# Neighbour sums on one core: the fourth group's first sums moved to the end of slot 4, and every result turned by VectorE

## The chip, the core and the metric

The kernel runs on one core of a Trainium2 chip. The metric is the device time of one execution in microseconds (us), taken as the median of several runs. The engines are TensorE (PE; its weight loads are listed apart as PEld), VectorE (DVE), ScalarE (ACT), GpSimd (POOL) and SyncE (SP, which here issues DMAs). Each engine runs its own instructions in the order in which the program lists them and waits on semaphores for what the others produce. SBUF is the on-chip memory, and PSUM holds the outputs of TensorE.

## The reference

For every edge, the feature row of its source node is added to the output row of its destination node. There are 4096 nodes with 128 features each in float32, and 65536 edges.

```python
output = np.zeros((num_nodes, dim), dtype=np.float32)
for i in range(len(edge_index_src)):
    output[edge_index_dst[i]] += node_features[edge_index_src[i]]
```

## The kernel before

**Tiling.** The nodes are 32 blocks of 128. The output is made in eight groups of 512 destinations (four blocks). For one group and one block of sources the kernel counts the edges between them in a 128 x 512 matrix `a`: DVE makes one-hot rows `oh` of the source and of the destination digits (`onehots`, line 804), PE multiplies them (`blocks`, line 817, into `psa`) and ACT copies the counts to SBUF (line 822). Then `product` (line 824) adds the block's features times `a` into `pso`, which holds 128 features x 512 destinations of the group; it takes two matmuls, since the features are split into a rounded part and a remainder. A **slot** is eight source blocks of one group, so a group has four slots and there are 32 slots (0 to 31).

**A slot on PE**, in order: `blocks` 0 to 3 of this slot, hook 2, `product` 4 to 7 of the slot before, `blocks` 4 to 7, hooks 3 and 4, `product` 0 to 3 of this slot, `finish`, hook 5. The one-hot rows of the next slot are written on DVE at the start of a slot, two buffers alternating: those of slot s + 2 need that the blocks of slot s are done, and PE cannot start slot s + 1 before DVE has written its rows.

**Sorting beside it.** The one-hot rows need the edges of each group sorted by source block. `pass2(g)` (line 625) does this for group g in steps hung on slots by a table of hooks (`at(slot, place, ...)`), so that they run between the slots of earlier groups: `buckets` (DVE, line 647), `chunk_sums` (POOL, lines 660 to 668, ends in the tile `four`), **`before_all`** (line 670: three matmuls of `four` with a triangular matrix into the PSUM tile `psb`, which ACT copies to `base`; these are the first sums that the title speaks of), `masked` and `folded` (POOL, multiply by `base` and add), `repeats` (DVE) and its folding (POOL), `ranks` (line 714: eight matmuls into `psr`, two ACT copies to `rank`), `permutations` (DVE, `p2a` or `p2c` from `rank`), `permuted` (PE, 48 matmuls `ps` of `p2a` with the payloads `v`), `take_pairs` (ACT) and `quad_keys` (DVE, the keys for the one-hot rows). `payloads` (POOL, `v`) of groups 2 to 6 is issued behind the next group's `chunk_sums`. `psb`, `psr` and `ps` share one PSUM buffer (tag `ps2`).

**At slot 4** two groups meet: hook 2 has `before_all`, `masked` and `folded` of group 3 (the fourth), hook 3 has `ranks` and `permutations` of group 2 (the third). Group 3's `buckets` and `chunk_sums` and group 2's `payloads` are hung on slot 2.

**Results.** When a group is complete, one slot later, ACT copies `pso` out (`evacuate`, line 375), and `finish` (line 391) turns it from features x destinations to destinations x features. For groups 0 and 2 (`BY_TENSOR`) PE turns it by four transposes into `psx`, ACT copies `psx` to `rows`, and one DMA of 256 KB stores it. For groups 1, 3, 4, 5 and 6 ACT copies `pso` to the PSUM tile `psx`, one DVE instruction turns its 32 x 32 blocks into `rows`, and four DMAs of 64 KB on SP's queue put the blocks in their places. Group 7 is turned at the very end (`leave`, line 408).

Of the kernel before, what the change touches and what calls it, by code (L numbers as in the profile page):

```python
# [8 lines left out]
P = 128  # L9
F32 = mybir.dt.float32  # L10
# [16 lines left out]
GROUPS = (4,) * 8  # L27
WARM = 38
LATE_PAYLOADS = (2, 3, 4, 5, 6)
BY_TENSOR = (0, 2)  # L30

WIN = ((0, 4, 0, 44), (4, 9, 0, 72), (9, 13, 8, 92), (13, 17, 16, 112), (17, NJ, 28, P))

# [44 lines left out]
def _fast(ctx, tc, X, src32, dst32, out, ident, fmax, flag_i, T):  # L78
    nc = tc.nc
    V, S, G, PE = nc.vector, nc.scalar, nc.gpsimd, nc.tensor  # L80
# [3 lines left out]
    sb1 = ctx.enter_context(tc.tile_pool(name="sb1", bufs=1))  # L84
    sb2 = ctx.enter_context(tc.tile_pool(name="sb2", bufs=2))
    ps = ctx.enter_context(tc.tile_pool(name="ps", bufs=2, space=bass.MemoryType.PSUM))
# [12 lines left out]
    for a, b in runs:  # L99
        at, n = 8 * sum(QN[:a]), 4 * QN[a]  # L100
        for queue, of, to in ((nc.sync, dst32, rawd), (nc.scalar, src32, raws)):
            queue.dma_start(
                out=to.rearrange("p (q n) w -> p q n w", q=NQ)[:, a:b, :n],
                in_=bass.AP(of, at, [[2 * T, P], [2 * n, b - a], [2, n], [1, 2]]))
# [268 lines left out]
    done = []  # L373

    def evacuate(k, pso):
        if k in BY_TENSOR:
            res = sb1.tile([P, 512], F32, name="res", tag="K1")
        else:
            res = ps.tile([P, 512], F32, name="psx", tag="misc", bufs=1)
        S.copy(out=res[:], in_=pso[:])  # L380
        done.append((k, res))

    def store_blocks(queues, rows, k):

        for a in range(4):
            queues[a % len(queues)].dma_start(
                out=out[4 * k * P:4 * (k + 1) * P, 32 * a:32 * (a + 1)].rearrange(
                    "(b j) f -> j b f", j=32),
                in_=rows[32 * a:32 * (a + 1)].rearrange("p (b f) -> p b f", f=32))

    def finish():
        for k, res in done:
            if k not in BY_TENSOR:
                rows = sb2.tile([P, 512], F32, name="rows", bufs=1)
                V.transpose(out=rows[:], in_=res[:])
                store_blocks((nc.sync,), rows, k)
                continue
            psx = ps.tile([P, 512], F32, name="psx", tag="misc", bufs=1)
            for i in range(4):
                PE.transpose(psx[:, i * P:(i + 1) * P], res[:, i * P:(i + 1) * P], ident[:])  # L400
            rows = sb2.tile([P, 4, P], F32, name="rows", bufs=1)
            S.copy(out=rows[:].rearrange("p i f -> p (i f)"), in_=psx[:])
            nc.sync.dma_start(
                out=out[4 * k * P:4 * (k + 1) * P, :].rearrange("(i p) f -> p i f", p=P),
                in_=rows[:])
        done.clear()

    def leave(k, pso):
# [209 lines left out]
    def at(slot, where, *fs):  # L618
        hooks.setdefault((slot, where), []).extend(fs)
# [5 lines left out]
    def pass2(g):  # L625
# [164 lines left out]
        f = 4 * g  # L790
        first_step = {3: (2, 4), 4: (6, 1)}.get(g, (f - 11, 1))
        at(*first_step, buckets, chunk_sums, owed.pop(g - 1, lambda: None))
        at(f - 8, 2, before_all, masked, folded)
        if g in LATE_PAYLOADS:
            owed[g] = payloads
        else:
            at(f - 8, 2, payloads)
        at(f - 7, 1, repeats, repeats_folded)
        at(f - 4, 5, ranks)
        at(f - 3, 1, lambda: permutations(0), lambda: permutations(1))  # L800
# [44 lines left out]
    def flag_of_all(fall):  # L845
# [3 lines left out]
                               op=OP.not_equal)  # L849

    buckets_1, payloads_1, column_sums_1, sums_1, counts_1 = pass2(1)
    buckets_2, chunk_sums_2 = pass2(2)
    for g in range(3, len(GROUPS)):
        pass2(g)

    V.tensor_copy(out=earlier[:, :, :4 * (NH - 1)].bitcast(F32),
                  in_=ones[:, :4 * (NH - 1)].bitcast(F32)[:, None].to_broadcast([P, 2, 2 * (NH - 1)]))
# [39 lines left out]
    for slot in range(slots):  # L897
# [21 lines left out]
        if slot > 1:  # L919
            for k in range(4, 8):  # L920
                product(k, *prev)
            if prev[0] % 4 == 3:
                evacuate(prev[0] // 4, prev[2])
# [4 lines left out]
        for k in range(4, 8) if slot == 0 else range(4):  # L928
            product(k, slot, a, pso)
        finish()  # L930
        do(slot, 5)
        prev = (slot, a, pso)
# [97 lines left out]
```

## Time and profile before

| what | value |
|---|---|
| median of 3 runs | 271.87 us (271.3 to 271.88) |
| profiled execution, its own time | 271.77 us |
| its span, first to last instruction | 270.2 us |
| PE busy | 252.3 us (93%) |
| DVE busy | 242.1 us (90%) |
| POOL busy | 197.0 us (73%), nothing after 212 us |
| ACT busy | 189.4 us (70%) |
| mean granted TensorE clock | 0.981 |

The last slots are PE's alone: PE works without a gap there. Earlier PE, DVE and POOL are all close to full, and which of them is waited for changes from slot to slot, so the table's shares do not say what a shorter piece of work is worth; the rows of the waits in order of time do.

### The profile page before, as it was taken

The numbers are of one execution on the slowest core, as the hardware profiler recorded it, in microseconds if no ns is written. First come the engines' busy times: TensorE is split into PE (matmuls) and PEld (weight loads), VectorE is DVE, ScalarE is ACT, GpSimd is POOL, SyncE is SP. The second block draws the span as 40 slices with busy tenths as digits, with TensorE's granted clock in tenths as the row PEclk, the third lists the DMA queues.
The fourth block names the chain that finished last, engine by engine and source line by source line (L and its number), as shares of the span: only waits on it lengthen the run. The fifth ranks groups of instructions, "written<-read, shape, count | busy, mean of one in ns | idle before, by whom it ended". The sixth has DMA issues, their size and how long they took to land.

```text
span 270.2 us, 7501 instructions
## 1 busy us (share of the span) xinstructions
PE 252.3 (93%) x3155; PEld 210.7 (78%) x3156; DVE 242.1 (90%) x270; ACT 189.4 (70%) x435; POOL 197.0 (73%) x205
## 2 busy tenths in 40 slices
PE   7899998989993999999899999999999999999991
PEld 7789997757882788778788887887888888878780
DVE  7999988999999199999999999999999989979801
ACT  3799898488763476676668687766876685868760
POOL 6499999999999996699999998999799300000000
PEclk9999999999998699999999999999999999999997
DMA  6910000000000010001000100200020020002002
GB/s 156 290 26 6 2 6 2 2 0 4 0 4 0 2 39 2 0 12 29 2 0 2 39 5 0 41 2 0 0 41 2 1 41 1 4 0 41 0 1 42
DMA packets 19556, 5.74 MB, mean 21 GB/s; under 512 B 12864, under 2 KB 19520, under 8 KB 19520
## 3 DMA queue, kind: packets, MB, share of 16 engines
q1 hardware_dynamic: 17648, 4.59, 7.7%
q10 hardware_dynamic: 1872, 0.66, 1.2%
q8 instruction: 25, 0.41, 0.6%
q14 instruction: 11, 0.09, 0.1%
HBM read 3.15 MB, written 2.10 MB: 19 GB/s over the span
## 4 chain that ended last, share of the span: by engine, by line
PE 54%; POOL 18%; DVE 17%; ACT 7%; issue 2%; DVEq 0%; POOLq 0%; ACTq 0%
PE pso L827 29%; PE psa L820 14%; DVE oh L242 10%; POOL cum L703 5%; ACT cum L284 4%; POOL xr L231 3%; POOL two L667 2%; POOL v L656 2%; PE ps L736 2%; PE psm L365 2%; PE psw L145 2%; POOL cum L710 1%; DVE oh L647 1%; POOL four L667 1%; DVE p2c L242 1%
## 5 line engine op out<-in xcount | busy, mean ns | idle before, releaser
L822 ACT CAST a<-psa 128x512 fp32r<-128x512 f32 x256 | 131.8, 604 | 31.8 <-PE psa L820 31.5
L827 PE MATMUL pso<-a,xr 128*128 128x512 f32 x512 | 136.3, 408 | 0.1
L827 PEld LDWEIGHTS pso<-a,xr 128*128 128x128 f32 x512 | 92.1, 191 | 17.4 <-ACT a L822 0.8
L242 DVE TENSOR_TENSOR oh<-psi,slo 128x4096 bf16<-128x4096 uint16 (+2 forms) x38 | 73.8, 1943 | 1.5 <-PE psa L820 1.5
L242 DVE TENSOR_TENSOR oh<-psi,dlo 128x4096 bf16<-128x4096 uint16 (+2 forms) x38 | 73.9, 1945 | 0.0
L820 PE MATMUL psa<-oh 128*128 128x128 bf16 x1024 | 68.8, 220 | 3.6 <-DVE oh L242 3.5
L820 PEld LDWEIGHTS <-oh 128*128 128x128 bf16 x1024 | 58.2, 98 | 17.7 <-issue 11.3
L656 POOL TENSOR_TENSOR v<-oh,sa 128x512 bf16<-128x512 bf16 x42 | 42.6, 1048 | 0.0
L703 POOL TENSOR_TENSOR cum<-oh,base 128x512 bf16<-128x512 bf16 x36 | 40.5, 1161 | 2.4 <-ACT base L678 2.4
L340 POOL TENSOR_TENSOR v<-oh,kab 128x704 f32<-128x704 bf16 x24 | 32.8, 1401 | 5.6 <-ACT kab L218 5.3
L242 DVE TENSOR_TENSOR p<-psi,rank 128x352 bf16<-128x352 uint16 (+5 forms) x60 | 26.0, 500 | 1.8 <-ACT rank L305 1.7
L667 POOL TENSOR_TENSOR two<-oh 128x512 bf16<-128x512 bf16 x18 | 20.4, 1160 | 4.2 <-DVE oh L647 4.2
L365 PE MATMUL psm<-v,p 128*128 128x64 bf16 x512 | 19.6, 193 | 0.9 <-DVE p L242 0.7
L242 DVE TENSOR_TENSOR p2a<-psi,rank 128x3072 bf16<-128x3072 uint16 (+2 forms) x14 | 14.2, 1062 | 5.9 <-ACT rank L724 5.9
L284 ACT ACTIVATE cum<-psc,sums 128x256 bf16<-128x256 f32 x50 | 19.1, 553 | 0.5 <-PE psc L281 0.5
L365 PEld LDWEIGHTS <-p 128*128 128x128 bf16 x512 | 17.1, 98 | 2.1 <-DVE p L242 1.7
L242 DVE TENSOR_TENSOR p2c<-psi,rank 128x3072 bf16<-128x3072 uint16 x8 | 13.6, 1745 | 0.0
L279 PE MATMUL psc<-early,oh 128*128 128x256 bf16 x67 | 13.2, 272 | 0.0
L647 DVE TENSOR_TENSOR oh<-psi,sbk 128x3072 bf16<-128x3072 uint16 (+3 forms) x9 | 12.5, 1393 | 0.0
L281 PE MATMUL psc<-early,oh 128*128 128x128 bf16 x67 | 12.1, 219 | 0.0
L710 POOL TENSOR_TENSOR cum<-cum 128x384 int32<-128x384 int32 x12 | 11.9, 1012 | 0.0
L535 ACT COPY ps<-ps 64x128 f32<-64x128 f32 x8 | 1.9, 235 | 13.8 <-issue 12.2
(117 smaller groups left out, 245.8 us busy)
## 6 DMA issues: line engine op xcount, KB each, us to landing
xf<-in_node_features_dram SPq DMA_DIRECT2D x4, 512.0 KB, 6.1
out_dram<-rows SPq DMA_DIRECT2D x22, 64.0 KB, 2.0
out_dram<-rows SPq DMA_DIRECT2D x2, 256.0 KB, 2.3
raw<-in_edge_index_src_dram ACTq DMA_DIRECT2D x1, 336.0 KB, 5.4
raw<-in_edge_index_dst_dram SPq DMA_DIRECT2D x1, 336.0 KB, 5.6
raw<-in_edge_index_src_dram ACTq DMA_DIRECT2D x2, 88.0 KB, 2.4
raw<-in_edge_index_dst_dram SPq DMA_DIRECT2D x2, 88.0 KB, 2.6
out_dram<-rows ACTq DMA_DIRECT2D x2, 64.0 KB, 2.9
```

The source lines that it names most:

```text
L242: V.tensor_tensor(out=dst.rearrange("p i (m k) -> p i m k", k=2), in0=io.rearrange("p i (m k) -> p i m k", k=2), in1=keys2[:, :, None, :]. ...
L284: S.activation(out=cum[:, 2 * i:2 * i + 2].rearrange("p j e -> p (j e)"), in_=psc[:, 2 * i * P:2 * (i + 1) * P], func=RELU, bias=bias)
L340: G.tensor_tensor(out=v1[q][:, l::4], in0=oh1q(q)[:, l::4], op=OP.mult, in1=kab[:, q, l::4, None].to_broadcast([P, NJ, NB]))
L365: PE.matmul(out=psm[:, l * 64:(l + 1) * 64], lhsT=t[:, j, l % 2, :], rhs=v1[q][:, 4 * j + l].bitcast(BF16), start=j == 0, stop=j == n - 1)
L647: V.tensor_tensor(out=T2["o"][:, c0:c1], op=OP.is_equal, in0=psi[:, 2].bitcast(U16).rearrange("p (s k) -> p s k", k=4)[:, None].to_broadca ...
L656: G.tensor_tensor(out=T2["v"][:, c:c + 4], in0=T2["o"][:, c:c + 4], op=OP.mult, in1=sa[:, c:c + 4, None, d0:d0 + 4].to_broadcast([P, 4, NB ...
L667: G.tensor_tensor(out=to[:, js], in0=of[:, js, 0], in1=of[:, js, 1], op=OP.add)
L703: G.tensor_tensor(out=flat("c")[:, c:c + 4], in0=flat("o")[:, c:c + 4], op=OP.mult, in1=T2["b"][:, c // NH, None].to_broadcast([P, 4, P]))
L710: G.tensor_tensor(out=t[:, cs, :n], in0=t[:, cs, :n], in1=t[:, cs, n:2 * n], op=OP.add)
L820: PE.matmul(out=psa[:, i * P:(i + 1) * P], lhsT=oh[:, 0, 4 * k + i, :], rhs=oh[:, 1, 4 * k + i, :], start=True, stop=True)
L822: S.copy(out=a[:, k, :], in_=psa[:])
L827: PE.matmul(out=pso[:], lhsT=xr[s // 16][:, s % 16, v, :], rhs=a[:, k, :], start=s == 0 and v == 0, stop=s == NB - 1 and v == 1)
```

## The change

`BY_TENSOR` and the branch for it are taken out of `evacuate` and `finish`: the results of groups 0 and 2 now go the way of the others (ACT copies to the PSUM tile `psx`, DVE turns, four DMAs of 64 KB). And for group 3 alone `before_all`, `masked` and `folded` move from hook 2 to hook 5 of slot 4.

```diff
-BY_TENSOR = (0, 2)
@@ evacuate
-        if k in BY_TENSOR:
-            res = sb1.tile([P, 512], F32, name="res", tag="K1")
-        else:
-            res = ps.tile([P, 512], F32, name="psx", tag="misc", bufs=1)
+        res = ps.tile([P, 512], F32, name="psx", tag="misc", bufs=1)
         S.copy(out=res[:], in_=pso[:])
         done.append((k, res))
@@ finish
         for k, res in done:
-            if k not in BY_TENSOR:
-                rows = sb2.tile([P, 512], F32, name="rows", bufs=1)
-                V.transpose(out=rows[:], in_=res[:])
-                store_blocks((nc.sync,), rows, k)
-                continue
-            psx = ps.tile([P, 512], F32, name="psx", tag="misc", bufs=1)
-            for i in range(4):
-                PE.transpose(psx[:, i * P:(i + 1) * P], res[:, i * P:(i + 1) * P], ident[:])
-            rows = sb2.tile([P, 4, P], F32, name="rows", bufs=1)
-            S.copy(out=rows[:].rearrange("p i f -> p (i f)"), in_=psx[:])
-            nc.sync.dma_start(
-                out=out[4 * k * P:4 * (k + 1) * P, :].rearrange("(i p) f -> p i f", p=P),
-                in_=rows[:])
+            rows = sb2.tile([P, 512], F32, name="rows", bufs=1)
+            V.transpose(out=rows[:], in_=res[:])
+            store_blocks((nc.sync,), rows, k)
@@ pass2
-        at(f - 8, 2, before_all, masked, folded)
+        after_sums = (f - 8, 5 if g == 3 else 2)
+        at(*after_sums, before_all, masked, folded)
         if g in LATE_PAYLOADS:
             owed[g] = payloads
         else:
-            at(f - 8, 2, payloads)
+            at(*after_sums, payloads)
```

The line numbers of the changed kernel are 1 lower up to `evacuate` and 13 or 14 lower behind `finish`. POOL's instructions keep their order.

PE in slot 4, before, from the last matmul of blocks 0 to 3 on (`psb` first sums, `pso` products, `psr` rank sums, `psx` the turned result of group 0):

```order
L820 MATMUL psa<-oh 128x128
L676 LDWEIGHTS before
L676 MATMUL psb<-four_2056,before 128x256
...
L827 MATMUL pso<-a,xr_177 128x512 x8
...
L720 MATMUL psr_2231<-same_1822,identb 128x96
L827 MATMUL pso<-a,xr_176 128x512 x8
L400 MATMUL psx<-ident,res 128x128 x4
L820 LDWEIGHTS oh
```

PE at the same place of the changed kernel:

```order
L807 MATMUL psa<-oh 128x128
L814 MATMUL pso<-a,xr_177 128x512 x8
...
L706 MATMUL psr_2214<-same_1822,identb 128x96
L814 MATMUL pso<-a,xr_176 128x512 x8
L662 LDWEIGHTS before
L662 MATMUL psb<-four_2056,before 128x256
...
L807 LDWEIGHTS oh
```

The first sums stand behind the rank sums and the last products of the slot, ahead of the first weights of slot 5, and the four transposes are gone.

ACT from slot 4 to slot 5, before (`a` are the counts' copies, `res` and `rows` the two copies of group 0's result):

```order
L822 CAST a<-psa 128x512 x12
L678 CAST base_2180<-psb 128x256
L380 COPY res<-pso 128x512
L822 CAST a<-psa 128x512 x4
L724 CAST rank_457<-psr_2231 128x96 x2
L402 COPY rows<-psx 128x512
L822 CAST a<-psa 128x512 x8
```

and in the changed kernel:

```order
L809 CAST a<-psa 128x512 x12
L376 COPY psx<-pso 128x512
L809 CAST a<-psa 128x512 x4
L710 CAST rank_457<-psr_2214 128x96 x2
L664 CAST base_2241<-psb 128x256
L809 CAST a<-psa 128x512 x8
```

The copy of the first sums stands behind the two rank copies, and one copy of the result is gone.

DVE from the rows of slot 5 to those of slot 6, before (`p2a` is the permutation of group 2):

```order
L242 TENSOR_TENSOR oh<-psi,slo_2077 128x4096
L242 TENSOR_TENSOR oh<-psi,dlo_2078 128x4096
L242 TENSOR_TENSOR p2a<-psi,rank_457 128x3072 x2
L242 TENSOR_TENSOR oh<-psi,slo_2077 128x4096
L242 TENSOR_TENSOR oh<-psi,dlo_2078 128x4096
```

and in the changed kernel:

```order
L241 TENSOR_TENSOR oh<-psi,slo_2077 128x4096
L241 TENSOR_TENSOR oh<-psi,dlo_2078 128x4096
L241 TENSOR_TENSOR p2a<-psi,rank_457 128x3072 x2
L390 STREAM_TRANSPOSE rows<-psx 128x512
L241 TENSOR_TENSOR oh<-psi,slo_2077 128x4096
L241 TENSOR_TENSOR oh<-psi,dlo_2078 128x4096
```

A turn stands ahead of the rows of slot 6; a second one, of group 2's result, stands in the same way ahead of the rows of slot 14.

## Rows read from the trace of the kernel before

**Rows 1.** Chain that ended last: start us, us, engine, output, line, count.

```profile
88.70 3.41 PE pso L827 x8
...
93.34 0.34 PE psr L720 x8
...
95.60 0.44 PE psx L400 x4
96.03 0.89 PE psa L820 x16
96.93 1.90 PE pso L827 x8
...
99.73 0.72 PE ps L736 x24
...
180.72 4.49 DVE oh L242 x2
185.26 1.07 PE psa L820 x16
```

**Rows 2.** Timeline of PE, slot 4: start, us, ..., count, [idle before, releaser].

```profile
82.51 1.07 PE L820 MATMUL psa<-oh 128*128 128x128 bf16 x16 [0.42 <-DVE oh L242]
87.90 0.80 PE L676 MATMUL psb<-four,before 128*128 128x256 bf16 x3 [4.32 <-POOL four L667]
```

**Rows 3.** Stretches: length, busy us (instructions) by engine, PEclk, DMA share, GB/s.

```profile
40.00:50.00 10.00, 8.78 (x216) 7.34 (x213) 8.33 (x23) 8.11 (x25) 10.00 (x10) 1.00 0.01 3
...
86.00:88.00 2.00, 0.10 (x1) 0.10 (x1) 2.00 (x2) 0.00 (x0) 2.00 (x4) 0.50 0.00 0
...
185.00:264.00 79.00, 78.74 (x748) 64.73 (x749) 67.34 (x47) 56.99 (x118) 25.10 (x26) 1.00 0.07 12
```

**Rows 4.** Timeline of ACT, slots 4, 8 and 12.

```profile
82.94 2.06 ACT L822 CAST a<-psa 128x512 fp32r<-128x512 f32 x4 [1.34 <-PE psa L820]
...
92.63 2.06 ACT L822 CAST a<-psa 128x512 fp32r<-128x512 f32 x4
94.53 0.47 ACT L724 CAST rank<-psr 128x96 bf16<-128x96 f32 x2
...
118.46 0.57 ACT L380 COPY psx<-pso 128x512 f32<-128x512 f32 x1 [0.46 <-PE pso L827]
...
144.00 0.58 ACT L380 COPY res<-pso 128x512 f32<-128x512 f32 x1 [0.44 <-PE pso L827]
```

**Rows 5.** Timeline of DVE, slots 4 to 12.

```profile
86.83 2.28 DVE L242 TENSOR_TENSOR oh<-psi,dlo 128x4096 bf16<-128x4096 uint16 x1
95.04 3.42 DVE L242 TENSOR_TENSOR p2a<-psi,rank 128x3072 bf16<-128x3072 uint16 x2 [5.93 <-ACT rank L724]
98.38 2.28 DVE L242 TENSOR_TENSOR oh<-psi,slo 128x4096 bf16<-128x4096 uint16 x1
...
119.43 0.71 DVE L395 STREAM_TRANSPOSE rows<-psx 128x512 f32<-128x512 f32 x1
120.06 2.26 DVE L242 TENSOR_TENSOR oh<-psi,slo 128x4096 bf16<-128x4096 uint16 x1
...
144.91 2.29 DVE L242 TENSOR_TENSOR oh<-psi,slo 128x4096 bf16<-128x4096 uint16 x1 [0.40 <-PE psa L820]
```

**Rows 6.** Timeline of POOL, 86 to 116 us.

```profile
86.07 1.77 POOL L667 TENSOR_TENSOR four<-two 128x384 bf16<-128x384 bf16 x2
87.81 6.08 POOL L656 TENSOR_TENSOR v<-oh,sa 128x512 bf16<-128x512 bf16 x6
...
110.15 3.40 POOL L667 TENSOR_TENSOR two<-oh 128x512 bf16<-128x512 bf16 x3 [4.16 <-DVE oh L647]
113.51 1.78 POOL L667 TENSOR_TENSOR four<-two 128x384 bf16<-128x384 bf16 x2
```

**Rows 7.** Timeline of PE in slot 8, the first sums of group 4.

```profile
116.09 0.49 PE L676 MATMUL psb<-four,before 128*128 128x256 bf16 x3
```

**Rows 8.** The page's list of DMA issues: queue, count, KB each, us to landing.

```profile
out_dram<-rows SPq DMA_DIRECT2D x22, 64.0 KB, 2.0
```

## The prediction, before the changed kernel was run

> **What bounds the kernel now.** I read the chain that ended last first, then the timelines of PE, DVE, ACT and POOL around slot 4, then the granted clock of the same stretch.
>
> The end belongs to PE: from 185 to 264 us it is busy for 78.74 of 79 us [rows 3], so whatever PE has gained when slot 19 starts at 185.26 is kept to the end. That start is released by DVE: DVE's pair of one-hot instructions of slot 19 starts at 180.72 and ends just ahead of it [rows 1]. So the question is by how much DVE will be earlier at 185 us.
>
> Back from there, DVE waits twice for long enough to matter: 5.93 us ahead of `p2a` at 95.04, for ACT's `rank`, and 0.40 us at 144.91, for PE [rows 5]. The 5.93 us are made in slot 4. PE ends blocks 0 to 3 of that slot and then stands 4.32 us in front of the first sums, until POOL has `four` at 87.84 [rows 2, 6]. All that follows in PE's order waits too, among it the rank sums that DVE needs, though POOL had made their inputs earlier (they stand ahead of `four` in its order). After the stall the granted clock is at 0.50, the lower level of 1.2 GHz [rows 3], and eight products take 3.41 us where they take 1.90 at the upper one [rows 1].
>
> **The change part by part.**
>
> *The first sums move behind the rank sums.* Up to 83.4 us nothing changes. I rebuild slot 4 from there at the upper clock. Blocks 0 to 3 start at 82.51 and take 0.89, so the products of slot 3 run from 83.40 to 85.30, blocks 4 to 7 to 86.19, the rank sums (0.34) to 86.53 and the products of slot 4 to 88.43 [rows 1, 2]. ACT copies group 0's result from 85.5 on (0.57, of which about 0.5 until the next may start), then four `a` copies until about 87.9 (92.63 to 94.53 is 1.90 a set) and `rank` until 88.4 (0.47) [rows 4]. The first sums use the PSUM buffer that the rank sums had, so PE must wait for the `rank` copies: 88.4, against PE's own 88.43, and `four` is there at 87.84 [rows 6]. The 4.32 us stall is gone, with nothing of size in its place.
>
> DVE then finds `rank` at 88.4, while it is still writing the rows of slot 5: 86.83 plus the spacing of 2.20 is 89.03 [rows 5]. `p2a` starts at 89.03 and not at 95.04: **6.01 us earlier**. The queue behind the moved work: ACT's `base` now waits for PE ahead of the copies of slot 5, which cannot start sooner anyway; POOL's `masked` needs `base` at 93.9, when its payloads end (87.81 + 6.08 [rows 6]), and `base` is there at about 89.4. PE starts slot 5 with DVE's rows at 89.1, waits again at about 93.5 for the last payload, which POOL has at 93.9 (`permuted`, 24 matmuls in 0.72 us from 92.9 on [rows 1]), and once more for the rows of slot 6. That is roughly 0.4, 0.5 and 0.8 us of waiting; it costs nothing, since DVE is the later one.
>
> *Group 0 is turned by DVE, in slot 4.* One turn takes 0.71 us, of which the spacing to the next instruction is 0.63 [rows 5]. It stands between `p2a` and the rows of slot 6, and DVE no longer waits there, so all of it is on the path: 6.01 − 0.63 = **5.38** at the rows of slot 6 (93.0 against 98.38). PE's four transposes (0.44 us [rows 1]) go from slot 4, where they would have stood in a wait for DVE, so I count nothing for them, and nothing for ACT's second copy.
>
> *POOL in slot 8.* POOL has waited 4.16 us for DVE's buckets of group 4 [rows 6]. DVE being 5.4 earlier, that wait is gone and POOL is earlier by 4.16, not by 5.4, since it then works without a gap. `four` of group 4 so ends at 115.29 − 4.16 = 111.13, while PE would reach its first sums at 116.09 − 5.4 = 110.7 [rows 6, 7]. PE waits 0.4 us there, is 4.95 earlier, and ACT's copy of group 1's result (118.46 + 0.57 [rows 4]) ends at 114.1. DVE's turn of group 1 would start at 119.43 − 5.38 = 114.05 and starts at about 114.15: **5.28** are left.
>
> *Group 2 is turned by DVE, in slot 12.* DVE waits there now for 0.40 us, until 144.91 [rows 5]. The copy of `pso` ends at 144.58 [rows 4], so in that frame the turn starts at 144.62 and the rows of slot 14 at 145.25, not 144.91: 0.34 us are lost, **4.94** are left. The bounds of this turn are 0 (wholly in the wait) and 0.72 (its full length); I take 0.34 since the rows of that very place give it. PE's second four transposes go from a stretch in which the next slots are released by DVE, so they give nothing. From there to slot 19 I find nothing that widens or narrows it.
>
> A rule of the Trainium skill speaks against this part: the page "VectorE: DVE Perf Modes", section "Rules for kernel authors", sends a 128 x 128 transpose to TensorE if PSUM will do as its destination. The rows agree in this place: TensorE's 0.44 us would lie in its waits, VectorE's 0.63 lies on the path in slot 4 and 0.34 in slot 12. By that rule, with the first part alone, PE would still meet `four` of group 4 in slot 8, so the 5.28 would stand, and slot 12 would take nothing: about 266.5. That is 0.34 us better than the whole change.
>
> *DMAs.* Eight of 64 KB take the place of two of 256 KB on SP's queue, where nothing else stands; they land after 2.0 us [rows 8], and the next turn needs `rows` only four slots (over 20 us) later. Nothing.
>
> **Sum.** 6.01 − 0.63 − 0.10 − 0.34 = 4.94 us. The profiled execution took 271.77, so 266.83; the median of the runs shown lies 0.1 above the profiled time. I say 266.9.
>
> **The rivals.**
>
> *PE gets back all it lost.* The stall (4.32), the slow products (3.41 − 1.90 = 1.51) and 0.44 of transposes are 6.3: 265.5. Against it: DVE has only 5.93 us of waiting to give there and gets 0.63 of new work, and slot 19 is released by DVE. Chance 0.06.
>
> *POOL becomes the bound.* If what POOL gains, 4.16, is all that the others gain (a later wait for `four` or `masked`), it is 267.6. For it: POOL is without a gap for long stretches. Against it: it reaches PE only in slot 8, and there it had 0.8 us in hand (115.29 to 116.09). Chance 0.08.
>
> *A short fall of the clock.* PE now has the three waits in and ahead of slots 5 and 6. If the lower level were granted for one slot, that slot would cost two times 1.5 us for its products and some tenths for its blocks, about 3.5; of it some 2.5 lie in the waits of slots 5 to 8, so about 1 is left: 267.8. Chance 0.05.
>
> *Slower: the clock stays low.* The place is slots 5 to 8, where PE waits for DVE in every slot. Each slot at 1.2 GHz costs 3.5 us; four make 14, less the 2.5 to 3 us of waits, so some 11 late against my forecast: about 278. It decides from about two slots on, where the cost passes the gain of 4.94 plus the waits. Against it: the clock stayed at 1.00 from 40 to 50 us with PE busy 8.78 of 10 [rows 3], and no wait that I find is near the 4.32 us after which it fell. Chance 0.04. The Trainium skill has this as a rule, in "TensorE: Matmul & The Clock Gate", section "A second HAM failure mode: psum-queue depth-cycling": a TensorE that idles briefly but often between groups of matmuls can swing between the two levels. The row of 40 to 50 us, with many such gaps, does not agree.
>
> *The change doesn't do what it says.* The stall could only move: the first sums would wait in the new place for `rank` or `four`. Both are there within 0.1 us of PE, so this is worth tenths, and the waits behind it hide them. If the whole stall came back, it would be the time of before, 271.9. Chance 0.02.
>
> **How the numbers follow.** The forecast of 266.9 has 0.75, the rivals 0.06, 0.08, 0.05, 0.04 and 0.02. The range goes from both turns at no cost (271.77 − 6.01 = 265.8, a tenth less for the runs' spread) to the short fall of the clock with 0.4 for that spread: 265.7 to 268.2. A change of 0.2%, 0.5 us, is about what a measurement of this kernel can tell from none. Faster 0.94, same 0.02, slower 0.04.
>
> **What would show it.** Right: no wait for `four` in slot 4, PEclk at 1.00 from 82 to 96 us, `p2a` at about 89.0, the rows of slot 6 at 93.0, POOL without its 4 us wait after 106, a PE wait of some 0.4 us for `four` of group 4 at about 110.7, slot 19 on PE at about 180.3. Wrong: a clock below 1.00 in slots 5 to 8, a wait of DVE for `rank` over 0.3 us, or a start of slot 19 off by over 0.6 us.

## The result and the profile after

The changed kernel took 266.91 us (median of four runs, 266.88 to 267.0), the kernel before 271.77 in the same comparison: a ratio of 0.9825, 95% interval 0.9808 to 0.9842. It is 4.9 us faster. The profiled execution of after took 266.95 us with a span of 265.4; PE's mean granted clock rose from 0.981 to 0.995.

On the page of after, the clock's row shows no dip (the 7 at its end stands on the page of before too and lies behind PE's last matmul), and PE is busy for less time in a shorter span:

```profile
PE 249.8 (94%) x3147; PEld 208.0 (78%) x3148; DVE 243.4 (92%) x272; ACT 188.5 (71%) x433; POOL 197.2 (74%) x205
...
PEclk9999999999999999999999999999999999999997
```

PE's timeline of after, slot 4 and the later starts that waited (start, us, what, count, idle before and its releaser):

```profile
82.61 1.07 PE L807 MATMUL psa<-oh 128*128 128x128 bf16 x16 [0.43 <-DVE oh L241]
83.49 2.09 PE L814 MATMUL pso<-a,xr 128*128 128x512 f32 x8
...
86.33 0.34 PE L706 MATMUL psr<-cum,identb 128*128 128x96 bf16 x4
...
88.59 0.50 PE L662 MATMUL psb<-four,before 128*128 128x256 bf16 x3
89.27 1.05 PE L807 MATMUL psa<-oh 128*128 128x128 bf16 x16 [0.18 <-DVE oh L241]
...
94.11 0.28 PE L722 MATMUL ps<-v,p2a 128*128 128x64 bf16 x4 [0.38 <-POOL v L642]
...
97.60 1.07 PE L807 MATMUL psa<-oh 128*128 128x128 bf16 x16 [0.54 <-ACT ps L523]
...
109.87 1.07 PE L807 MATMUL psa<-oh 128*128 128x128 bf16 x16 [0.85 <-DVE oh L241]
111.31 0.49 PE L662 MATMUL psb<-four,before 128*128 128x256 bf16 x3 [0.38 <-POOL four L653]
...
129.97 1.07 PE L807 MATMUL psa<-oh 128*128 128x128 bf16 x16 [0.48 <-DVE oh L241]
...
180.34 1.07 PE L807 MATMUL psa<-oh 128*128 128x128 bf16 x16 [0.48 <-DVE oh L241]
```

Where PE stood 4.32 us [rows 2] it now goes straight on: the products of slot 3 start at 83.49, the rank sums at 86.33 (93.2 before), and the first sums at 88.59 without a wait. The new waits of slots 5, 6 and 8 are 0.18, 0.38, 0.54 and 0.38 us; the 0.85 us ahead of slot 8 is not new (0.84 before). Slot 19 starts at 180.34 against 185.26 [rows 1].

The stretches that answer to [rows 3] (length, busy us by engine, PEclk): the clock stays at the upper level where it had fallen to 0.50, and from slot 19 on PE works without a gap as before.

```profile
86.00:88.00 2.00, 2.00 (x23) 1.78 (x21) 2.00 (x2) 2.00 (x5) 2.00 (x4) 1.00 0.03 8
...
180.00:259.00 79.00, 78.66 (x748) 64.67 (x749) 67.42 (x47) 56.97 (x118) 25.21 (x26) 1.00 0.07 12
```

DVE's timeline of after:

```profile
86.94 2.28 DVE L241 TENSOR_TENSOR oh<-psi,dlo 128x4096 bf16<-128x4096 uint16 x1
89.14 3.41 DVE L241 TENSOR_TENSOR p2a<-psi,rank 128x3072 bf16<-128x3072 uint16 x2
92.46 0.70 DVE L390 STREAM_TRANSPOSE rows<-psx 128x512 f32<-128x512 f32 x1
93.09 2.25 DVE L241 TENSOR_TENSOR oh<-psi,slo 128x4096 bf16<-128x4096 uint16 x1
...
114.29 0.72 DVE L390 STREAM_TRANSPOSE rows<-psx 128x512 f32<-128x512 f32 x1
...
139.48 0.72 DVE L390 STREAM_TRANSPOSE rows<-psx 128x512 f32<-128x512 f32 x1
140.12 2.25 DVE L241 TENSOR_TENSOR oh<-psi,slo 128x4096 bf16<-128x4096 uint16 x1
...
164.66 0.72 DVE L390 STREAM_TRANSPOSE rows<-psx 128x512 f32<-128x512 f32 x1
```

`p2a` follows the rows of slot 5 without the wait of 5.93 us [rows 5]; the turn of group 0 stands behind it and holds the rows of slot 6 for 0.63 us.

POOL's timeline of after shows the other wait gone: 106.12 follows 104.42 + 1.75 at once, where POOL had waited 4.16 us [rows 6].

```profile
86.22 1.79 POOL L653 TENSOR_TENSOR four<-two 128x384 bf16<-128x384 bf16 x2
...
104.42 1.75 POOL L684 TENSOR_TENSOR same<-same 128x480 bf16<-128x480 bf16 x2
106.12 3.40 POOL L653 TENSOR_TENSOR two<-oh 128x512 bf16<-128x512 bf16 x3
109.48 1.78 POOL L653 TENSOR_TENSOR four<-two 128x384 bf16<-128x384 bf16 x2
```

Its `four` of group 4 ends at 111.26, and PE's first sums of slot 8 start at 111.31: in that slot PE follows POOL.

### The profile page after: what moved, and what is told of

Read it like the earlier page. It is cut to its first block, busy times and chain, and to the rows that moved or that the text cites. A ratio compares the mean times of both kernels' runs of the same rounds, so it can differ in the third digit from the quotient of the medians.

```text
span 265.4 us, 7496 instructions
## 1 busy us (share of the span) xinstructions
PE 249.8 (94%) x3147; PEld 208.0 (78%) x3148; DVE 243.4 (92%) x272; ACT 188.5 (71%) x433; POOL 197.2 (74%) x205
## 4 chain that ended last, share of the span: by engine, by line
PE 39%; POOL 37%; DVE 11%; ACT 7%; issue 3%; DMA 1%; SPq 0%; DVEq 0%; POOLq 0%
PE pso L814 21%; POOL cum L689 10%; PE psa L807 10%; POOL v L642 9%; DVE oh L241 6%; POOL two L653 5%; ACT cum L283 4%; POOL xr L230 3%; POOL four L653 3%; POOL cum L696 3%; PE psm L364 2%; POOL same L684 2%; POOL cum L698 2%; DVE p2c L241 1%; DVE p L241 1%
## 5 line engine op out<-in xcount | busy, mean ns | idle before, releaser
L814 PE MATMUL pso<-a,xr 128*128 128x512 f32 x512 | 134.6, 404 | 0.1
L814 PEld LDWEIGHTS pso<-a,xr 128*128 128x128 f32 x512 | 91.0, 189 | 17.1 <-ACT a L809 0.8
```

Source lines behind the costliest of these rows:

```text
L814: PE.matmul(out=pso[:], lhsT=xr[s // 16][:, s % 16, v, :], rhs=a[:, k, :], start=s == 0 and v == 0, stop=s == NB - 1 and v == 1)
```

## The experiments

The theory is that of the prediction. The rivals are that DVE's work simply adds up, that PE's own waits count, and that the turns on DVE help.

### Which turn costs what

Four kernels ran side by side: the changed kernel, the first part alone, and the change with one of the two groups turned by TensorE. The edits, on the kernel before with the first sums moved:

```diff
 part1_alone:   BY_TENSOR = (0, 2)
 g0_by_tensor:  BY_TENSOR = (0,)
 g2_by_tensor:  BY_TENSOR = (2,)
```

> The changed kernel itself, beside the three that follow. Both theories: 266.9 us, as measured before.

> Only the first sums move; the results of groups 0 and 2 are still turned by TensorE. Theory of the prediction (in slot 8 POOL's first sums of group 4 cap the gain, so that the turn of group 0 is hidden behind that wait, and only the turn of group 2 costs 0.34): 266.5 us. Rival (both turns add to DVE's path one for one, 0.63 and 0.34): 265.9 us.

> The changed kernel, but group 0 turned by TensorE. Theory of the prediction (the cap by POOL in slot 8 holds): 266.8 to 266.9 us, no gain though 0.63 us of DVE work are gone. Rival (DVE's work adds up): 266.3 us.

> The changed kernel, but group 2 turned by TensorE. Theory of the prediction: 266.5 us, and the same as the run with both on TensorE. Rival (DVE's work adds up): 266.6 us, and 0.6 above that run.

Measured, as medians of five runs beside 271.82 for the kernel before: 266.97, 266.64, 266.68 and 266.44. The four lie within 0.53 us. The turn of group 0 by DVE instead of TensorE adds 0.29 us in one pair (266.97 − 266.68) and takes off 0.20 in the other (266.44 − 266.64), where the rival wanted 0.6 in both and the theory nothing. So the times speak against the rival, but they do not show where the turn goes. The traces do. The first part alone: PE's first sums of slot 8, DVE's turn of group 1 and the rows of slot 14, where DVE waits 0.40 us for PE as in the kernel before.

```profile
111.15 0.49 PE L676 MATMUL psb<-four,before 128*128 128x256 bf16 x3 [0.99 <-POOL four L667]
```

```profile
114.14 0.72 DVE L395 STREAM_TRANSPOSE rows<-psx 128x512 f32<-128x512 f32 x1 [0.70 <-ACT psx L380]
...
139.61 2.29 DVE L242 TENSOR_TENSOR oh<-psi,slo 128x4096 bf16<-128x4096 uint16 x1 [0.40 <-PE psa L821]
```

Group 0 turned by TensorE, DVE's turn of group 1:

```profile
114.15 0.72 DVE L395 STREAM_TRANSPOSE rows<-psx 128x512 f32<-128x512 f32 x1 [0.73 <-ACT psx L380]
```

Without the turn of group 0, DVE gets to slot 8 0.6 us earlier and then waits 0.70 or 0.73 us for ACT's copy, which hangs on PE, which waits 1.0 us for POOL. The turn of group 1 starts at 114.14 or 114.15 where it started at 114.15 in the changed kernel's run of this comparison. So the turn of group 0 is hidden behind POOL. The turn of group 2 is not: from the start of slot 4's blocks to slot 19 PE takes 97.79 us in the two kernels where DVE turns group 2 (180.23 − 82.44 in both) and 97.51 and 97.55 where TensorE does (179.96 − 82.45, 180.08 − 82.53). It costs 0.24 to 0.28 us, against 0.34 in the prediction. The rival, by which the turn of group 0 adds its whole 0.63, falls.

What is left of the times lies behind the last matmul. From the start of the last turn on DVE to the end of the span, these four executions took 5.8, 5.7, 5.5 and 5.5 us. Only the last four DMAs and the program's end stand there; the last section tells where they differ.

### The second part alone

The kernel before with `BY_TENSOR = ()`: DVE turns all results, and the first sums stay where they were.

> Only the turns go to DVE; the first sums stay in front of the rank sums. Theory of the prediction: the stall and the low clock of slot 4 stay, DVE has 0.63 more in slot 4 and 0.34 more in slot 12: 272.7 us. Rival (turns by DVE are free or help, since PE and ACT lose work): 271.3 to 271.8 us.

Measured: 272.75 us, ratio 1.0037 (1.0024 to 1.0051): slower by 0.9 us. DVE's timeline shows that the wait for `rank` is what it was and that the turn comes on top of it; the row of POOL is that of slot 8:

```profile
95.01 3.42 DVE L242 TENSOR_TENSOR p2a<-psi,rank 128x3072 bf16<-128x3072 uint16 x2 [5.92 <-ACT rank L724]
98.35 0.71 DVE L395 STREAM_TRANSPOSE rows<-psx 128x512 f32<-128x512 f32 x1
```

```profile
110.72 3.41 POOL L667 TENSOR_TENSOR two<-oh 128x512 bf16<-128x512 bf16 x3 [4.26 <-DVE oh L647]
```

Here POOL waits for DVE, so nothing hides the turn of group 0, and both count: the rows of slot 6 start 0.60 us later than in the kernel before (98.98 against 98.38), those of slot 14 0.92 later (145.83 against 144.91). The two parts do not add: the second costs 0.9 us alone and about 0.3 beside the first.

### How much of it is the clock

The kernel before, with PE kept at work while it waits:

```diff
+        if g == 3:
+            at(f - 8, 2, lambda: keep_busy(70))
         at(f - 8, 2, before_all, masked, folded)
```

> The kernel before, with 70 dummy matmuls of 128 columns (about 4 us, results unused) ahead of the first sums, where PE stands. The wait for POOL stays as long, but PE is kept at work. Theory of the prediction (the 6.01 us of DVE are about 4 of waiting for POOL and about 2 of products at the lower clock behind it): PEclk stays at 1.00, rank 2.0 us earlier, 269.8 us. Rival (the clock's part is hidden): 271.8 us.

Measured: 269.95 us, ratio 0.9936 (0.9921 to 0.9951): 1.9 us less, with the first sums as late as before. PE's timeline, then DVE's, then the stretch behind the stall, here and, in the last row, in the kernel before:

```profile
83.62 4.07 PE L145 MATMUL psw<-ones 128*128 128x128 bf16 x70
87.94 0.49 PE L676 MATMUL psb<-four,before 128*128 128x256 bf16 x3 [0.25 <-POOL four L667]
```

```profile
93.20 3.42 DVE L242 TENSOR_TENSOR p2a<-psi,rank 128x3072 bf16<-128x3072 uint16 x2 [4.05 <-ACT rank L724]
```

```profile
88.00:90.00 2.00, 2.00 (x11) 1.56 (x10) 1.15 (x1) 0.37 (x1) 2.00 (x3) 1.00 0.00 0
...
88.00:90.00 2.00, 2.00 (x7) 1.58 (x7) 1.11 (x1) 0.37 (x1) 2.00 (x3) 0.50 0.00 0
```

`p2a` starts at 93.20 instead of 95.04 with the clock at 1.00. So of the 6.0 us by which the change moves `p2a`, 1.9 are the products and blocks that PE ran at the lower clock behind the stall, and 4.1 the wait itself.

### Is it PE's waiting or DVE's?

The changed kernel with the first sums one hook earlier, straight behind the rank sums:

```diff
-        after_sums = (f - 8, 5 if g == 3 else 2)
+        after_sums = (f - 8, 3 if g == 3 else 2)
```

> The changed kernel, but the first sums stand straight behind the rank sums, ahead of the slot's last products. PE must there wait about 1.9 us for the rank copies (shared PSUM buffer), but DVE gets its rank as early. Theory of the prediction (DVE is the later one, PE's waits there cost nothing): 266.9 to 267.1 us. Rival (PE's waiting counts): 268.8 us.

Measured: 266.85 us, ratio 0.9821 (0.9806 to 0.9836), the same as the change. PE's first sums and its starts of slots 6 and 8, DVE's `p2a`, and the stretch behind the wait:

```profile
88.48 0.50 PE L662 MATMUL psb<-four,before 128*128 128x256 bf16 x3 [1.70 <-ACT rank L710]
...
97.77 1.05 PE L807 MATMUL psa<-oh 128*128 128x128 bf16 x16
...
109.81 1.07 PE L807 MATMUL psa<-oh 128*128 128x128 bf16 x16 [0.65 <-DVE oh L241]
```

```profile
89.08 3.42 DVE L241 TENSOR_TENSOR p2a<-psi,rank 128x3072 bf16<-128x3072 uint16 x2
```

```profile
88.00:90.00 2.00, 1.52 (x9) 1.28 (x10) 2.00 (x2) 0.80 (x4) 2.00 (x3) 1.00 0.03 8
```

PE stands 1.70 us and nothing is lost. PE is the later one for a while: it starts slot 6 without a wait, some 0.2 us later than in the change, as counted from the blocks of slot 4 (97.77 − 82.56 against 97.60 − 82.61 and, in the second trace of the change, 97.43 − 82.44). By slot 8 it has caught up and waits for DVE again, 0.65 us instead of 0.85. The clock stays at 1.00 after this wait. What brought the gain is that the rank sums go ahead of the wait, not that PE waits less.

### Taking the cap away

First sums of group 4 moved too, in slot 8, from hook 2 to hook 3, and groups 0 and 2 on TensorE:

```diff
-        at(f - 8, 2, before_all, masked, folded)
+        after_sums = (f - 8, {3: 5, 4: 3}.get(g, 2))
+        at(*after_sums, before_all, masked, folded)
```

> Groups 0 and 2 turned by TensorE, the fourth group's first sums at the end of slot 4, and the fifth group's first sums moved too, in slot 8, from hook 2 to hook 3, behind the second half of the blocks, so that PE no longer meets POOL there. Theory of the prediction: the cap of slot 8 is gone, DVE keeps all 6.01 us: 265.8 us. Rival (the cap is elsewhere): 266.5 us, as with the first part alone.

> The run with both first sums moved, again, beside the one before it: 265.8 us by both theories.

Measured: 265.80 us and, beside the next one, 265.83; ratios 0.9784 (0.9771 to 0.9797) and 0.9782 (0.9768 to 0.9795). PE meets `four` without a wait, and DVE's turn of group 1 starts 0.75 us earlier than with the first part alone (PE's rows, then DVE's, of the second execution):

```profile
112.84 0.49 PE L676 MATMUL psb<-four,before 128*128 128x256 bf16 x3
...
129.06 1.07 PE L821 MATMUL psa<-oh 128*128 128x128 bf16 x16 [0.71 <-DVE oh L242]
```

```profile
113.39 0.70 DVE L395 STREAM_TRANSPOSE rows<-psx 128x512 f32<-128x512 f32 x1
```

So the cap was POOL in slot 8. This kernel is 1.1 us faster than the change. From the blocks of slot 4 to slot 19 PE takes 96.72 us here (179.20 − 82.48) against 97.51 with the first part alone, so 0.8 us of it is the cap; most of the rest is the turn of group 2.

### What is late next

The same kernel with `BY_TENSOR = (0, 1, 2)`:

> As the run with both first sums moved, but group 1 is turned by TensorE too, so that DVE loses another turn, in slot 8. Theory (DVE is then earlier than PE at slot 11, where PE had 0.71 us in hand, less 0.44 for its transposes; PE becomes the bound, and the gain over that run is some 0.2 to 0.25 us): 265.55 us, and PE no longer waits for DVE at the start of slot 11. Rival (DVE stays the bound and keeps its whole 0.63): 265.2 us, with PE still waiting for DVE there.

Measured: 264.77 us, ratio 0.9742 (0.9729 to 0.9755), the fastest of all: 1.06 us below the run before it, where 0.2 to 0.25 (theory) and 0.6 (rival) were expected. PE's timeline, then the last of DVE's one-hot instructions for slot 11:

```profile
115.02 0.60 PE L400 MATMUL psx<-ident,res 128*128 128x128 f32 x4
...
128.47 1.07 PE L821 MATMUL psa<-oh 128*128 128x128 bf16 x16
...
178.62 1.07 PE L821 MATMUL psa<-oh 128*128 128x128 bf16 x16 [0.48 <-DVE oh L242]
```

```profile
126.11 2.28 DVE L242 TENSOR_TENSOR oh<-psi,dlo 128x4096 bf16<-128x4096 uint16 x1
```

The sign that the theory named is there: PE no longer waits for DVE at slot 11. But the two meet there almost at once: DVE's rows are complete at 128.39 and PE starts at 128.47, so PE is at most some hundredths the later one, and the size is the rival's. Slot 11 starts 0.59 us earlier (129.06 − 128.47), and slot 19 0.58 earlier (179.20 − 178.62). I had taken the idle time of 0.71 us for PE's reserve; but that is counted from the modelled end of the last product, and from one start to the next there is 0.16 us more, and the 48 `ps` matmuls ahead of slot 10 took 1.45 us from start to start where they had taken 1.61. The remaining 0.5 us of the 1.06 are again behind the last turn: 5.2 us to the end of the span, against 5.7.

## Why the prediction was right, point by point

- **The stall goes, and `p2a` starts at 89.0.** Right: 89.14, in an execution that stands 0.10 us later already at the blocks of slot 4 (82.61 against 82.51). From those blocks on, `p2a` came 6.00 us earlier; 6.01 was forecast.
- **The first sums find `rank` and `four` there.** Right: no wait at 88.59.
- **PE then waits 0.4, 0.5 and 0.8 us in and ahead of slots 5 and 6.** Right in kind, too long in size: 0.18, 0.38 and 0.54.
- **The clock stays up.** Right; the rivals of a falling clock did not happen, with PE waits of up to 0.85 us in slots 4 to 19 of the changed kernel and of 1.70 in an experiment. The low level of before was read from the stretch of 86 to 88 us, which lies inside the stall; the row of 88 to 90 us in the experiment on the clock shows that it held behind the stall too.
- **The turn of group 0 takes 0.63, the rows of slot 6 come 5.38 earlier.** Right: 5.39 (98.38 − 93.09 + 0.10).
- **POOL loses its wait, and PE waits some 0.4 us for `four` in slot 8.** Right: 0.38. The two runs in which group 0 is turned by TensorE show that this is a cap and not a sum: the 0.63 and the 0.10 of the forecast are one term, 0.73 us. The turn of group 0 is on DVE's path in slot 4, as forecast, but it does not reach slot 19 (97.79 us from the blocks of slot 4 with either engine).
- **The turn of group 2 loses 0.34.** Nearly: 5.24 earlier at the turn of group 1, 4.89 at the rows of slot 14 (144.91 − 140.12 + 0.10), so 0.35 there. But the step behind it, "from there to slot 19 I find nothing that widens or narrows it", was wrong by about 0.1: in the kernel before DVE had waited for ACT's copy in slot 16, and since DVE has gained a little less than PE up to there, it does not wait now. This is the row of before:

```profile
169.57 0.72 DVE L395 STREAM_TRANSPOSE rows<-psx 128x512 f32<-128x512 f32 x1 [0.17 <-ACT psx L380]
```

  At the same turn of after (164.66) no wait is listed, and slot 19 starts 5.02 us earlier counted from the blocks of slot 4, not 4.94. Two losses outside the sum offset it: the 0.10 us ahead of slot 4 and 0.1 behind the last turn.
- **The DMAs: "Nothing".** Not quite: the stretch behind the last turn is 5.8 us against 5.7, for the reason in the last section.
- **266.9 us.** The sum gave 4.94 us and the profiled executions differ by 4.82; the term of group 2 was about 0.1 too large, and the two losses above were not in the sum. That the median, 266.91, meets the forecast to 0.01 us is luck; that it lies within some tenths is not.
- **The rule on transposes.** By the Trainium skill ("VectorE: DVE Perf Modes", section "Rules for kernel authors") TensorE should have kept the two turns. In this kernel the runs agree: the second part alone is 0.9 us slower, and the two fastest kernels have two and three results turned by TensorE. For group 0 beside POOL's cap it made no difference up to slot 19.
- **"PE gets back all it lost".** It did not, as argued: DVE still releases slot 19 (0.48 us of idle PE ahead of 180.34).

## What to carry to other kernels

Where two independent sums queue on one engine, the one whose input comes last belongs at the back: its wait costs every instruction behind it, and here also the lower clock for the products that follow. To price such a step, carry the shift forward engine by engine and stop at each place where another engine is just in time: the gain is the smallest shift that these places let through, not the length of the stall. And an operation on the busier engine can be hidden today and count in full once the cover is gone: the turn of group 0 costs 0.63 us alone and nothing beside POOL's cap.

## What I had not expected of the hardware

The stretch behind the last turn, with the same four DMAs of 64 KB in every kernel, took between 5.2 and 5.8 us in the twelve traces, and it goes by kernel rather than by run: 5.8 us in the four traces where TensorE turns no result, 5.7 in the five where it turns two, 5.5 in the two where it turns one, and 5.2 in the one where it turns three.

The traces show where it goes. SP ends the program by waiting for twelve semaphores, always in the same order, the last eight of them set by DMAs. Where a semaphore is already set, the next wait comes 0.06 us later; from the last wait to the end of the span 0.93 us pass in every trace. In all but the fastest kernel the last store lands 4.42 to 4.47 us behind the start of the turn. What differs is the place of its semaphore in SP's order: where TensorE turns no result it is the first of the eight, so that seven more waits stand behind it, with two results it is the third, with one the sixth. In the fastest kernel the first of the eight is met at 3.84 us, and the last store lands at 4.15, before SP gets to its semaphore; why it lands earlier there, the one trace does not show. SP's wait for DMAs, in the changed kernel and in the fastest (us in total, times, longest):

```profile
SPq L1012 <- DMA out_dram<-rows: 2.1, 1, 2.1
...
SPq L1026 <- DMA out_dram<-rows: 1.4, 1, 1.4
```

So kernels can differ by up to 0.6 us in the end of the program alone, about half of it by the order of these waits (5.8 against 5.5 us). A comparison of kernels by less than that is better made on the start of the last undisturbed stage than on the total.
